# One core, a decoder layer with 32 experts: the overflow branch is named ahead of the first gather

## The chip, the core and the metric

The kernel runs on one core of a Trainium2 chip. A core has five engines that run their own instruction streams in order and meet through semaphores: TensorE (PE, with its weight loads shown as PEld), VectorE (DVE), ScalarE (ACT), GpSimd (POOL) and SyncE (SP), which here only issues transfers. The metric is the device time of one execution in microseconds; the kernel before takes 2275.43 us (median of three runs, 2272.79 to 2275.65).

## The reference

One decoder layer over 2048 tokens of width 1024. Only its mixture of experts is touched here:

```python
h2 = rmsnorm(x, g_ffn[i])
x = x + hier_moe(h2, ...)       # 32 experts: top-1 of 4 groups, then top-2 of its 8 experts
# inside: rows of ht are gathered by expert, in blocks of one expert each
return (jax.nn.silu(xb @ w_eg[e]) * (xb @ w_eu[e])) @ w_ed[e]
# and the rows of each token are summed again, weighted by the router
```

Ahead of it stand a state-space mixer, a windowed attention and their output projection; behind it a gated per-layer embedding and a last RMSNorm.

## The kernel before

All products are made in float32 accuracy out of rounded pieces: each operand is split into a high part, cast by ScalarE (L1488 for weights, L1375 for the gathered rows), and a low part, subtracted by VectorE (L1489 and L1376). A weight unit is 128 x 2048 floats, 1 MB; an expert has six, e0_0 to e0_5 for the expert in place 0, of which 0 to 3 are gate and up and 4 and 5 are down. A unit is loaded by SyncE (`moe_raw`, L1479) into one of four raw buffers and split (`moe_split`) into one of six slots.

The router (`route_tables`) leaves a table of row numbers, `IDX`, and the number of overflow blocks, `NOV`. Places alternate between wide ones, of 128 rows plus up to 96 more (place 0 gathers `s0` and `s32`), and narrow ones of 128 rows (place 31 gathers `s31`). `fetch` calls `moe_in` (L1360 on) for each gather: GpSimd gathers rows by an indirect transfer into one of two buffers `xg` (L1364), TensorE transposes them (L1374), ScalarE and VectorE split them into `xw` (L1375, L1376). The trace calls the gathered tile `xgs`, the transposes `txs`, the expert's raw, high and low weights `e_r`, `e_h` and `e_l`, whatever the place.

`overflow` (L1562 on) holds a branch and a loop over blocks that did not fit; with these inputs there are none, so every engine jumps over the loop. Having jumped, each engine adds to its semaphores what the loop would have added, so that what stands behind the loop and shares a buffer with it (the slots 3 to 5, a raw buffer, an `xg` buffer, two PSUM buffers) waits until the other engine has jumped as well. An engine's stream is not reordered across the branch where a buffer is shared.

What stands in which place of a stream is decided when the program is built, by a scheduler with a timeline of its own. It takes the instructions in the order in which the code names them, moves them where it finds them free earlier, and keeps the order of two users of the same buffer. The engines then run their streams strictly as built.

The first matmuls of the experts are those of `moe_gu_wide` (L1413, L1414): `ws` out of e0_0 and the first half of `xw`, for 224 rows.

Of the kernel before, what the change touches and what calls it, by code (L numbers as in the profile page):

```python
# [43 lines left out]
def more(r):  # L44

    return 32 * ((r < R1) + (r < R3) + (r < R2))


class Kern:
# [1451 lines left out]
    def moe(self):  # L1501
        nc = self.nc
        self.yb_d = self.scratch("yb_d", [2 * T + 1, 1024])

        p = self.mp
        for q in "hl":
            p.tile([128, 8, 128], F32R, tag=f"x{q}", name=f"x{q}at", bufs=1)
        p.tile([128, 512], F32, tag="act", name="aat", bufs=3)
        for q in "hl":
            p.tile([128, 4, 128], F32R, tag=f"a{q}", name=f"a{q}at", bufs=2)  # L1510
        p.tile([128, 4, 2 * RM], F32R, tag="aw", name="awat", bufs=1)
        order = []
        for i in range(16):
            order += [(i, [i, 32 + i]), (31 - i, [31 - i])]

        def number(r):
            return nc.sync.value_load(self.EID[0:1, r:r + 1], min_val=0, max_val=NE - 1)

        def fetch(slots):
            ix = [self.IDX[:, s:s + 1] for s in slots]  # L1520
            if len(slots) == 1:
                return self.moe_in(ix[0], f"s{slots[0]}"), 128
            m = more(slots[0])
            x = self.mp.tile([128, 8, 2, RM], F32R, tag="xw", name=f"xw{slots[0]}", bufs=1)[:, :, :, 0:128 + m]
            for q, (s, w) in enumerate(zip(slots, (128, m))):
                self.moe_in(ix[q], f"s{s}", w, x, 128 * q)
            return x, 128 + m

        self.wslots((), range(3))
        with self.tc.issue_after(self.stored):  # L1530
            v = number(0)
            ahead = [self.moe_raw((v, j), f"e0_{j}") for j in range(3)]
        cur = v, fetch(order[0][1])
        self.wslots(range(3), ())

        with self.tc.issue_after(self.routed[0]), self.tc.issue_after(self.routed[1]):
            ahead = [self.moe_split(w, f"e0_{j}") for j, w in enumerate(ahead)]
        self.wslots(range(3, 6), (3,))
        self.overflow()
        self.rctx.close()  # L1540
        self.wslots((3, 4, 5, 0, 1, 2), range(4))
        prev = None
        for n, (r, slots) in enumerate(order):
            v, xs = cur
            if n + 1 < len(order):
                cur = number(order[n + 1][0]), fetch(order[n + 1][1])
            nm = [f"s{s}" for s in slots]
            wt = ahead + [self.moe_unit((v, j), f"e{r}_{j}") for j in range(len(ahead), 4)]
            ahead = []
            x, rows = xs  # L1550
            wide = rows > 128
            acts = self.moe_gu_wide(x, rows, wt, nm[0]) if wide else self.moe_gu(x, wt, nm[0])
            if prev is not None:
                self.moe_down(*prev())
            hl = acts if wide else self.moe_act(acts, nm[0])

            def prev(v=v, r=r, hl=hl, slots=slots, nm=nm):
                wt = [self.moe_unit((v, j), f"e{r}_{j}") for j in (4, 5)]
                return hl, wt, [self.YDX[:, s:s + 1] for s in slots], nm
        return self.moe_down(*prev())  # L1560
# [231 lines left out]
```

## Time and profile before

| what | value |
| --- | --- |
| median of three runs | 2275.43 us |
| the profiled execution's own time | 2276.06 us |
| its span, first to last instruction | 2274.3 us |
| TensorE busy | 2202.4 us, 97% |
| VectorE busy | 1651.0 us, 73% |
| ScalarE busy | 1208.2 us, 53% |
| GpSimd busy | 364.3 us, 16% |
| mean granted TensorE clock | 0.988 |

The shares of busy time are means over stages of different kinds, so the profile is read by stage: the router's end and the first expert lie between 1276 and 1312 us after the span's start, the experts as a whole between 1297 and 2010 us. A row of a timeline gives start, duration, engine, line, operation, what is written and read, and in brackets the engine's idle time before it with what ended it. A name with a q behind it (PEldq, SPq) is that engine's sequencer: register loads, branches, semaphores and the issue of transfers.

### The profile page before, as it was taken

To read this page: it belongs to the slowest core of one execution; us is meant where nothing else is said; L and a number is where in the kernel's file an instruction comes from. 1 tells how busy PE (TensorE), PEld (TensorE's weight loads), DVE (VectorE), ACT (ScalarE), POOL (GpSimd) and SP (SyncE) were. 2 spreads that over 40 slices of the span, in tenths; PEclk is the share of its full clock that TensorE was granted. 3 is DMA by queue.
4 is the path that set the end of the run, shared out by engine and by line. 5 is a ranking of instruction groups with operands and counts; after the bars stand their busy time and mean duration, and the time that the engine had idled before them with its cause. 6 is when DMAs were issued, how large, how long until landed. Compare 5 with 4: busy or idle time off the path is not lost. (4 is left out here: it accounts for less than half of the span.)

```text
span 2274.3 us, 38003 instructions
## 1 busy us (share of the span) xinstructions
PE 2202.4 (97%) x14524; PEld 1994.3 (88%) x14524; DVE 1651.0 (73%) x2923; ACT 1208.2 (53%) x2011; POOL 364.3 (16%) x281
## 2 busy tenths in 40 slices
PE   8889999999999999999999799999999999999997
PEld 8888997899999999998887688888988888887875
DVE  7978646788786534435666687788888888887997
ACT  6433335567675423322222576666677767774443
POOL 0033200211111000000001211222212222210212
PEclk9989999999999999999999899999999999999998
DMA  8485554643433656645553788889889988986562
GB/s 315 140 278 182 154 153 133 239 156 120 144 126 128 222 165 196 199 135 163 168 167 115 290 306 295 312 324 342 316 314 337 352 325 320 341 298 234 211 203 93
DMA packets 135322, 512.51 MB, mean 225 GB/s; under 512 B 16417, under 2 KB 34769, under 8 KB 107745
## 3 DMA queue, kind: packets, MB, share of 16 engines
q1 hardware_dynamic: 112544, 429.56, 55.3%
q0 software_dynamic: 22448, 80.23, 9.4%
q8 instruction: 115, 1.88, 0.3%
q14 instruction: 71, 0.57, 0.1%
q10 hardware_dynamic: 144, 0.26, 0.0%
HBM read 405.51 MB, written 101.20 MB: 223 GB/s over the span
## 5 line engine op out<-in xcount | busy, mean ns | idle before, releaser
L1489 DVE TENSOR_TENSOR e_l<-e_r,e_h 128x2048 fp32r<-128x2048 f32 x192 | 438.1, 2289 | 136.9 <-ACT e_h L1488 136.1
L1488 ACT CAST e_h<-e_r 128x2048 fp32r<-128x2048 f32 x192 | 366.7, 1911 | 136.0 <-PE ws L1413 40.2
L1413 PE MATMUL ws<-xw,e_h 128*128 128x320 f32 (+2 forms) x1024 | 289.9, 359 | 6.6 <-PEq L1566 6.6
L1414 PE MATMUL ws<-xw,e_l 128*128 128x160 f32 (+2 forms) x1024 | 251.6, 248 | 0.0
L1413 PEld LDWEIGHTS ws<-xw,e_h 128*128 128x128 f32 x1024 | 191.8, 188 | 10.5 <-issue 6.8
L1414 PEld LDWEIGHTS ws<-xw,e_l 128*128 128x128 f32 x1024 | 195.5, 191 | 0.0
L1364 POOL DMA_INDIRECT xgs<-h_d,rt x48 | 87.0, 1812 | 392.6 <-PE txs L1374 366.1
L1464 POOL DMA_INDIRECT yb_d<-yos,rt x48 | 79.1, 1648 | 211.8 <-DVE yos L1460 111.3
L839 POOL TENSOR_TENSOR s<-s,m 128x1024 f32<-128x1024 f32 (+1 forms) x32 | 59.7, 1865 | 313.9 <-DVE m L838 248.1
L77 PE MATMUL pz<-pg_h,pl 128*128 128x512 f32 (+1 forms) x264 | 103.5, 393 | 2.9 <-DVE pl L1627 2.8
L75 PE MATMUL pz<-pg_h,ph 128*128 128x512 f32 (+1 forms) x264 | 102.2, 387 | 0.9 <-ACT ph L1626 0.9
L76 PE MATMUL pz<-pg_l,ph 128*128 128x512 f32 (+1 forms) x264 | 102.0, 386 | 0.0
L75 PE MATMUL gus<-e_h,xhs 128*128 128x512 f32 x256 | 101.3, 396 | 0.0
L77 PE MATMUL gus<-e_h,xls 128*128 128x512 f32 x256 | 101.1, 395 | 0.0
L76 PE MATMUL gus<-e_l,xhs 128*128 128x512 f32 x256 | 99.8, 390 | 0.0
L75 PE MATMUL u<-xh,u_h 128*128 128x256 f32 x256 | 72.3, 288 | 11.3 <-ACT u_h L96 8.3
L836 ACT ACTIVATE s<-s,m 128x256 f32<-128x256 f32 (+1 forms) x128 | 62.8, 492 | 25.4 <-DVE m L832 25.0
L76 PE MATMUL u<-xl,u_h 128*128 128x256 f32 x256 | 72.8, 288 | 3.2 <-DVE xl L422 3.2
L77 PE MATMUL u<-xh,u_l 128*128 128x256 f32 x256 | 72.2, 285 | 0.0
L924 ACT ACTIVATE gt<-gz,bgate 128x256 f32<-128x256 f32 x128 | 53.5, 470 | 28.7 <-PE gz L77 24.0
L1671 POOL TENSOR_TENSOR pth<-pth,gtail 128x1024 f32<-128x1024 f32 x15 | 36.4, 2425 | 176.4 <-ACT pth L1670 151.6
L77 PEld LDWEIGHTS pz<-pg_h,pl 128*128 128x128 f32 x264 | 49.9, 189 | 15.5 <-DVE pl L1627 6.5
(1488 smaller groups left out, 7348.0 us busy)
## 6 DMA issues: line engine op xcount, KB each, us to landing
e_r<-in_We SPq DMA_DIRECT2D x192, 1024.0 KB, 7.3
m_d<-mo SPq DMA_DIRECT2D x64, 256.0 KB, 4.2
yg<-yb_d SPq DMA_DIRECT2D x15, 1024.0 KB, 7.5
xt<-in_xT SPq DMA_DIRECT2D x16, 512.0 KB, 8.7
sq<-in_x SPq DMA_DIRECT2D x16, 512.0 KB, 4.8
m<-m_d SPq DMA_DIRECT2D x16, 512.0 KB, 5.4
xr<-in_x SPq DMA_DIRECT2D x16, 512.0 KB, 4.4
x_d<-xr POOLq DMA_DIRECT2D x16, 512.0 KB, 3.2
```

Of the source, the lines that this page charges most:

```text
L75: mm(out, ah, bh, start=start, stop=False)
L76: mm(out, ah, bl, start=False, stop=False)
L77: return mm(out, al, bh, start=False, stop=stop)
L836: A.activation(s[:, i], s[:, i], AF.Exp, bias=m[:, i:i + 1], accum_out=dn[:, i:i + 1])
L839: nc.gpsimd.tensor_tensor(out=s, in0=s, in1=dn.unsqueeze(2).to_broadcast([128, 4, n]), op=ALU.mult)
L924: A.activation(th[:, m], z[:, m], AF.Tanh, bias=bg[:, q:q + 1], scale=0.5)
L1364: nc.gpsimd.indirect_dma_start(out=xg[0:rows], out_offset=None, in_=self.h2_d[:], in_offset=bass.IndirectOffsetOnAxis(ap=idx[0:rows], axis=0))
L1413: mm(acc[b].rearrange("p (a n) -> p a n", a=2), wh[:, c:c + 128], xk, start=s, stop=False)
L1414: mm(acc[b][:, 0:n], wl[:, c:c + 128], xk[:, 0], start=False, stop=e)
L1464: nc.gpsimd.indirect_dma_start(out=self.yb_d[:], out_offset=bass.IndirectOffsetOnAxis(ap=d[0:rows], axis=0), in_=yo[0:rows], in_offset=None)
L1488: nc.scalar.copy(hi, raw)
L1489: nc.vector.tensor_tensor(out=lo, in0=raw, in1=hi, op=ALU.subtract)
```

## The change

The code names the overflow branch right behind the loads of the first three units, then the gathers of place 0, then the splits of e0_0 to e0_2.

```diff
@@ -1530,13 +1530,13 @@
         with self.tc.issue_after(self.stored):
             v = number(0)
             ahead = [self.moe_raw((v, j), f"e0_{j}") for j in range(3)]
+        self.wslots(range(3, 6), (3,))
+        self.overflow()
         cur = v, fetch(order[0][1])
         self.wslots(range(3), ())
 
         with self.tc.issue_after(self.routed[0]), self.tc.issue_after(self.routed[1]):
             ahead = [self.moe_split(w, f"e0_{j}") for j, w in enumerate(ahead)]
-        self.wslots(range(3, 6), (3,))
-        self.overflow()
         self.rctx.close()
         self.wslots((3, 4, 5, 0, 1, 2), range(4))
         prev = None
```

No instruction is added or removed. SyncE's stream is the same up to the end of the expert stage. On ScalarE, at the end of the router, the four casts of the gathered rows of place 0 (out of `txs00` to `txs321`) stand ahead of the branch in the kernel before; behind the loop (the dots) come two casts of weights, e0_3 and e31_0, and then copies of results:

```order
L1077 COPY po15_14556<-pp151_14565 128x512
L1375 CAST xw0_14614<-txs00_14617 128x4x128
L1375 CAST xw0_14614<-txs01_14624 128x4x128
L1375 CAST xw0_14614<-txs320_14633 128x4x96
L1375 CAST xw0_14614<-txs321_14640 128x4x96
L1565 TENSOR_LOAD rt35_14398
L1566 COMPARE_AND_BRANCH
...
L1566 UNCONDITIONAL_BRANCH
L1488 ACT_TABLE_LOAD
L1488 CAST e0_3_h_14927<-e0_3_r_14925 128x2048
L1488 CAST e31_0_h_15152<-e31_0_r_15150 128x2048
L1420 COPY ts000_15000<-ws000_14932 128x224
```

In the changed kernel ScalarE's stream at the same place, behind the loop, reads:

```order
L1566 UNCONDITIONAL_BRANCH
L1488 ACT_TABLE_LOAD
L1488 CAST e0_3_h_14927<-e0_3_r_14925 128x2048
L1488 CAST e31_0_h_15152<-e31_0_r_15150 128x2048
L1375 CAST xw0_14852<-txs00_14855 128x4x128
L1375 CAST xw0_14852<-txs01_14862 128x4x128
L1488 CAST e31_1_h_15158<-e31_1_r_15156 128x2048
L1375 CAST xw0_14852<-txs320_14871 128x4x96
L1375 CAST xw0_14852<-txs321_14878 128x4x96
L1375 CAST xhs31_14909<-txs310_14911 128x512
```

The casts of the first gathered rows have moved behind the branch, and behind casts of three weight units whose loads are issued after SyncE's own jump. The casts of e0_0 to e0_2 stand ahead of the branch in both. VectorE's stream has the same form; behind the loop it reads, in the changed kernel:

```order
L1566 UNCONDITIONAL_BRANCH
L1489 TENSOR_TENSOR e0_3_l_14928<-e0_3_r_14925,e0_3_h_14927 128x2048
L1489 TENSOR_TENSOR e31_0_l_15153<-e31_0_r_15150,e31_0_h_15152 128x2048
L1376 TENSOR_TENSOR xw0_14852<-txs00_14855,xw0_14852 128x4x128
L1376 TENSOR_TENSOR xw0_14852<-txs01_14862,xw0_14852 128x4x128
L1489 TENSOR_TENSOR e31_1_l_15159<-e31_1_r_15156,e31_1_h_15158 128x2048
L1376 TENSOR_TENSOR xw0_14852<-txs320_14871,xw0_14852 128x4x96
L1376 TENSOR_TENSOR xw0_14852<-txs321_14878,xw0_14852 128x4x96
```

The four subtractions for `xw` stood ahead of the branch before; now two stand behind the second weight subtraction and two behind the third. On TensorE and GpSimd nothing but the four groups of transposes and the two gathers of place 0 has passed the branch; the gather of `s32` now uses the `xg` buffer that the loop uses.

## Rows read from the trace of the kernel before

**Rows 1.** The page's head and first part: span, busy time of the engines

```profile
span 2274.3 us, 38003 instructions
PE 2202.4 (97%) x14524; PEld 1994.3 (88%) x14524; DVE 1651.0 (73%) x2923; ACT 1208.2 (53%) x2011; POOL 364.3 (16%) x281
```

**Rows 2.** Busy time by stretch, the experts from their first matmul

```profile
core 0: us, PE busy (x) PEld busy (x) DVE busy (x) ACT busy (x) POOL busy (x), PEclk, DMA share, GB/s
1297.20:2010.00 712.80, 712.76 (x4132) 626.68 (x4133) 578.65 (x678) 498.40 (x623) 154.56 (x89) 1.00 0.89 325
```

**Rows 3.** TensorE's longest wait from 1297 us on: total, times, longest

```profile
PE ws L1413 <- PEq L1566: 6.6, 1, 6.6
```

**Rows 4.** Timeline of TensorE from the router's last matmuls to the experts

```profile
1277.36 1.48 PE L1341 MATMUL sm<-rt,rt 128*128 128x96 bf16 x31 [0.17 <-ACT rt L1336]
1286.35 1.94 PE L1374 MATMUL txs<-ident,xgs 128*128 128x128 f32 x8 [7.51 <-DMA xgs<-h_d,rt]
1289.15 1.51 PE L1374 MATMUL txs<-ident,xgs 96*128 96x96 f32 x8 [0.86 <-DMA xgs<-h_d,rt]
1297.24 0.71 PE L1413 MATMUL ws<-xw,e_h 128*128 128x448 f32 x1 [6.58 <-PEq L1566]
...
1300.24 0.37 PE L1413 MATMUL ws<-xw,e_h 128*128 128x448 f32 x1
```

**Rows 5.** The branch, line 1566: durations in ns, first and last start

```profile
L1566 PEldq COMPARE_BRANCH  x1: 6786/6786/6786, 1290.3 to 1290.3; - x1
L1566 ACTq COMPARE_BRANCH  x1: 50/50/50, 1291.2 to 1291.2; - x1
...
L1566 PEldq EVENT_SEMAPHORE  x1: 51/51/51, 1297.1 to 1297.1; - x1
```

**Rows 6.** Timeline of ScalarE around the branch

```profile
1290.70 0.48 ACT L1375 CAST xw<-txs 128x384 fp32r<-128x384 f32 x1 [0.16 <-PE txs L1374]
1297.25 1.28 ACT L1488 ACT_TABLE_LOAD   x1 [6.07 <-PEq L1566]
1298.55 3.71 ACT L1488 CAST e_h<-e_r 128x2048 fp32r<-128x2048 f32 x2
...
1307.89 1.92 ACT L1488 CAST e_h<-e_r 128x2048 fp32r<-128x2048 f32 x1
```

**Rows 7.** Timeline of VectorE around and behind the branch

```profile
1290.57 1.20 DVE L1376 TENSOR_TENSOR xw<-txs,xw 128x384 fp32r<-128x384 f32 x2 [0.94 <-ACT xw L1375]
1300.48 4.49 DVE L1489 TENSOR_TENSOR e_l<-e_r,e_h 128x2048 fp32r<-128x2048 f32 x2 [8.71 <-ACT e_h L1488]
...
1309.84 2.29 DVE L1489 TENSOR_TENSOR e_l<-e_r,e_h 128x2048 fp32r<-128x2048 f32 x1 [1.43 <-ACT e_h L1488]
...
1312.35 1.28 DVE L1376 TENSOR_TENSOR xls<-txs,xhs 128x512 fp32r<-128x512 f32 x2
```

**Rows 8.** Weight loads: first issue, those of 1288 to 1293 us, landing times

```profile
1287.42 53.66 SPq L1479 DMA_DIRECT2D e_r<-in_We  x15
...
L1479 SPq DMA_DIRECT2D e_r<-in_We x1: 815/815/815, 1288.0 to 1288.0; - x1
DMA to landing us min/median/max: 10.9/10.9/10.9
...
L1479 SPq DMA_DIRECT2D e_r<-in_We x2: 332/332/333, 1289.1 to 1292.6; - x2
...
DMA to landing us min/median/max: 5.6/7.1/10.9
```

**Rows 9.** Busy time by stretch around the first matmul, columns as in rows 2

```profile
1295.00:1300.00 5.00, 2.76 (x9) 2.61 (x10) 0.00 (x0) 2.73 (x2) 0.93 (x1) 0.50 1.01 418
1300.00:1305.00 5.00, 5.00 (x33) 4.74 (x33) 4.49 (x2) 2.26 (x2) 0.00 (x0) 0.98 0.91 343
```

**Rows 10.** Gathers on GpSimd: that of s32, and the first behind TensorE's jump

```profile
1283.15 1.83 POOL L1364 DMA_INDIRECT xgs<-h_d,rt  x1 [0.30 <-issue]
...
1297.46 0.93 POOL L1364 DMA_INDIRECT xgs<-h_d,rt  x1 [5.58 <-PEq L1566]
```

## The prediction

> **What bounds the kernel now.** I read the page's first part, then busy time by stretch, then the list of waits from the experts on, then the timelines of the engines around the branch. TensorE is busy for 2202.4 of 2274.3 us [rows 1]. From the first expert matmul at 1297.24 us to 2010 us it is busy for 712.76 of 712.80 us [rows 2], and the longest entry in its list of waits from 1297 us to the end is the one just ahead of that first matmul, 6.6 us in one piece [rows 3]. So the experts run on TensorE alone, without a gap: a microsecond by which their first matmul starts later or earlier goes through to the end. The whole question is when that matmul starts.
>
> Before, it starts at 1297.24. TensorE ends the router's matmuls at 1277.36 + 1.48 = 1278.84, waits 7.5 us for the first gather, transposes from 1286.35 to 1290.66, and then jumps over the overflow loop, which holds its sequencer from 1290.3 for 6.786 us [rows 4, 5]. The last subtraction for the gathered rows ends at 1290.57 + 1.20 = 1291.77 [rows 7], 5.5 us ahead of the matmul. So the jump is the last of these waits: two waits, for the gather and for the jump, stand one behind the other.
>
> **The change part by part.** *The jump.* It now follows the router's matmuls directly, while TensorE would wait for rows anyway: 1278.84, less the 0.4 us by which the sequencer began its jump ahead of the end of the last transposes (1290.3 against 1290.66) [rows 4, 5], plus 6.8 is 1285.3, a microsecond ahead of the first gather's landing. By itself this removes up to 6.6 us [rows 3]. If the jump is as short as ScalarE's, 0.05 us [rows 5], it ends earlier still; neither case is on the path found below.
>
> *The gathers.* The first has its row numbers at the same time as before, and the other `xg` buffer. The second, of `s32`, now takes the buffer that the loop uses, so it waits until TensorE has jumped; a gather that waited so was issued at 1297.46, 0.36 us behind the semaphore at 1297.1 [rows 5, 10]. That makes about 1285.6 instead of 1283.15 [rows 10].
>
> *The casts and subtractions of the gathered rows.* This is the term that decides. They used to stand ahead of the branch, where nothing but routing work preceded them. In the new streams of ScalarE and VectorE, two of the four stand behind the splits of e0_3 and e31_0, and two behind the split of e31_1 as well. Those three units are loaded by SyncE, whose stream is unchanged, from 1287.42 on [rows 8]. Queued behind the waiting casts are, in turn, VectorE's subtractions, the second pair of transposes (which need the PSUM buffers of the first pair) and the first expert matmul. The price, step by step:
>
> - e31_0 is issued at 1288.0 and lands 10.9 us later, at 1298.9; it is the second load of that batch [rows 8].
> - Its cast takes 1.9 us (3.71 for two) [rows 6]: 1300.8. VectorE's subtraction, 2.29 [rows 7]: 1303.1.
> - Two subtractions of gathered rows, 1.28 for such a pair [rows 7]: 1304.4. Now the PSUM buffers are free for the transposes of `s32`, some 0.75 us for each half (1.51 for both) [rows 4], with a cast of 0.48 behind each [rows 6]; these run while VectorE does the next step.
> - VectorE subtracts e31_1, 2.29: 1306.7. That unit must have landed and been cast by 1304.4. It is issued at 1289.1, right behind e31_0 [rows 8], and 1 MB at 343 to 418 GB/s [rows 9] is 2.5 to 3.1 us: it lands at 1301.4 to 1302.0, and with 1.92 for the cast [rows 6] it is ready by 1303.9.
> - The first of the two subtractions of 96 rows, 0.6 (1.20 for two) [rows 7]: 1307.3. From its release to the first matmul I take 0.1, as from the semaphore at 1297.1 to 1297.24 [rows 4, 5]: 1307.4.
>
> So the first matmul starts 1307.4 - 1297.24 = 10.2 us later. ScalarE adds a little: it must first have e0_3, with a table load of 1.28 and a cast of 1.9 [rows 6]. If that load lands 2.5 to 3.1 us ahead of e31_0, at 1295.8 to 1296.4, the cast of e31_0 begins at 1299.0 to 1299.6 instead of 1298.9. I add 0.5. The sum is +10.7 us.
>
> *The splits of e0_0 to e0_2.* The code names them later, but on ScalarE and VectorE they stand ahead of the branch as before, and their raw buffers come free at the same times. Price 0; the cover is the wait for the gather, some 7.5 us [rows 4].
>
> *What is late next.* When TensorE does start, e0_0 to e0_3, e31_0 and e31_1 are already split, three units more than before, where e31_1 was cast only at 1307.89, 10.7 us behind the first matmul [rows 6]. I see no new gap: TensorE had none with less in hand [rows 2].
>
> *Bounds of what the trace doesn't show.* The loads could be quicker: with the fastest landing near here, 5.6 us [rows 8], e0_3 is there at 1293.0, and the same chain (1.28, 1.9, 1.9, 2.29, 1.28, 2.29, 0.6, 0.1) ends at 1304.6, +7.4 us. The clock could give something back: before, the granted clock was 0.50 (1.2 GHz) in 1295 to 1300 [rows 9], after little work since 1278.84, and the first matmul took 0.71 us where one at 1300.24 took 0.37 [rows 4]; running 3.0 us at that level costs at most half of it, 1.5. TensorE will again have been nearly idle, so I take 0 of this back, and -1.5 as the end: +5.9 in all. On the other side, the gather of `s32`, 96 x 4 KB = 0.39 MB, now runs among the weight loads, 0 to 1.1 us at 343 GB/s; I take 0, since one gather of 0.5 MB, the one issued at 1297.46 [rows 10], leaves the same stretch. And the trace proves e31_1 landed only by 1307.89 [rows 6]; if it really lands that late, its cast, subtraction and the rest (1.92, 2.29, 0.6, 0.1) end at 1312.8, +15.6 us.
>
> Against the profiled execution's own 2276.06 us (span 2274.3 and 1.8 around it) the sum is 2286.8. That execution lies 0.6 above the median of the runs, 2275.43, so the forecast is 2286.1, rounded to 2286.
>
> **The rivals.** *Faster: the jump is hidden and nothing takes its place.* The place is TensorE's jump. With the gather of `s32` issued at 1285.6 and the 8.6 us that it took before from issue to the last subtraction (1283.15 to 1291.77) [rows 7, 10], the first matmul starts at 1294.3, 2.9 us earlier; with a short jump that no longer holds the gather, at 1291.9, 5.3 us earlier: 2270 to 2273, middle 2271. The point from which it decides: e31_1 must be split before VectorE would subtract the last 96 rows, at 1290.6. For it speaks that the two waits are in series now [rows 4]; against it, that e31_1 is issued only at 1289.1 and the fastest landing here took 5.6 us [rows 8]. Chance 0.04.
>
> The Trainium skill, on its page "Runtime: NRT & Kernel Launch", section "Instruction fetch mechanics", says that a taken branch with a target outside the prefetched window stalls until its page has been fetched. By that rule the jump's length is a fetch that can be laid under any wait, which is this rival. The trace agrees for TensorE (6.786 us against 0.05 on ScalarE [rows 5]) but says nothing of who waits next.
>
> *No change: slack.* The later start could be made up in a stage that waits for something else. Against it: 0.04 us of idle time in 713 [rows 2]. For it: only that three more units are split at the start. 2275.4; chance 0.05.
>
> *Much slower: e31_1 lands late*, or another load pushes itself ahead of it, since the fourth load of the batch, issued at 1292.6 [rows 8], waits for VectorE's jump, which now comes earlier. Up to +15.6, so 2291. Chance 0.10.
>
> *It doesn't do what it says.* For the splits this is so, and priced at 0; the gathers do move.
>
> **How the numbers follow.** Forecast (+5.9 to +14.5 us) 0.81, late 0.10, no change 0.05, faster 0.04. The range 2281 to 2290 is the forecast's: its low end is the bound +5.9, its high end lies short of the late case, and some 0.19 is left out. What a measurement of this kernel can tell from no change is 0.2%, 4.6 us. Slower 0.91, same 0.05, faster 0.04.
>
> **What would show it.** In the new profile: TensorE's jump ahead of the first transposes, ending by 1287; the casts of `xw` on ScalarE behind two casts of weights, at about 1301, where the engine's idle time ends with a landing load; a first L1413 matmul at 1307 to 1308, its wait put down to VectorE's L1376; no gap on TensorE from there to 2010 + 11 us. A first matmul ahead of 1303, a gap later in the experts, or splits of e31_0 done before 1299 would prove the sum wrong.

## The result, and the profile after

The changed kernel takes 2287.43 us (median of five runs, 2283.76 to 2291.13) against 2275.43 us; the ratio is 1.0054, with a 95% interval of 1.0039 to 1.0068, or 12.3 us (8.9 to 15.5). The forecast was 2286, within 2281 to 2290, and slower.

The page's head, as [rows 1]: the span is 11.3 us longer, and TensorE's busy time 3 us.

```profile
span 2285.6 us, 38010 instructions
...
PE 2205.4 (96%) x14524; PEld 1996.7 (87%) x14524; DVE 1649.9 (72%) x2923; ACT 1207.6 (53%) x2011; POOL 366.1 (16%) x281
```

TensorE's list of waits from 1276 us to the end, its longest entries first (total, times, longest). [rows 3] is the same list from 1297 us on:

```profile
PE txs L1374 <- DVE xw L1376: 15.4, 1, 15.4
PE txs L1374 <- DVEq L1566: 7.8, 1, 7.8
...
PE ws L1413 <- DVE xw L1376: 1.7, 1, 1.7
```

The wait for TensorE's own jump is gone from the list. In its place stands one of 15.4 us for VectorE's L1376, the subtractions of gathered rows. The timeline of TensorE, as [rows 4], shows where:

```profile
1275.83 1.48 PE L1341 MATMUL sm<-rt,rt 128*128 128x96 bf16 x31 [0.17 <-ACT rt L1336]
1285.15 1.94 PE L1374 MATMUL txs<-ident,xgs 128*128 128x128 f32 x8 [7.84 <-DVEq L1566]
1302.53 1.54 PE L1374 MATMUL txs<-ident,xgs 96*128 96x96 f32 x8 [15.44 <-DVE xw L1376]
1305.79 0.74 PE L1413 MATMUL ws<-xw,e_h 128*128 128x448 f32 x1 [1.72 <-DVE xw L1376]
...
1309.31 0.38 PE L1413 MATMUL ws<-xw,e_h 128*128 128x448 f32 x1
```

The router's last group starts 1.5 us earlier than in the trace of before. That place moves from 1272 to 1278 us over the traces of this study, whose TensorE streams are alike ahead of it, so I count from it. From the start of that group to the first expert matmul is called the lead-in here: 1305.79 - 1275.83 = 29.96 us, against 1297.24 - 1277.36 = 19.88 before [rows 4]. That is +10.08 us. The second pair of transposes, once 0.9 us behind the first, now waits for PSUM buffers that VectorE frees only at 1302.5.

ScalarE, as [rows 6], and VectorE, as [rows 7], in the order in which their streams have it:

```profile
1294.15 1.28 ACT L1488 ACT_TABLE_LOAD   x1 [11.07 <-DMA e_r<-in_We]
1295.45 3.87 ACT L1488 CAST e_h<-e_r 128x2048 fp32r<-128x2048 f32 x2
1299.22 1.06 ACT L1375 CAST xw<-txs 128x512 fp32r<-128x512 f32 x2
1300.18 1.91 ACT L1488 CAST e_h<-e_r 128x2048 fp32r<-128x2048 f32 x1
1303.47 0.48 ACT L1375 CAST xw<-txs 128x384 fp32r<-128x384 f32 x1 [1.38 <-PE txs L1374]
```

```profile
1297.38 4.49 DVE L1489 TENSOR_TENSOR e_l<-e_r,e_h 128x2048 fp32r<-128x2048 f32 x2 [12.54 <-ACT e_h L1488]
1301.79 1.28 DVE L1376 TENSOR_TENSOR xw<-txs,xw 128x512 fp32r<-128x512 f32 x2
1302.99 2.28 DVE L1489 TENSOR_TENSOR e_l<-e_r,e_h 128x2048 fp32r<-128x2048 f32 x1
1305.18 1.01 DVE L1376 TENSOR_TENSOR xw<-txs,xw 128x384 fp32r<-128x384 f32 x2
```

ScalarE stands idle for 11.07 us until a weight unit lands; that is e0_3, the first that its stream asks for. The first transposes of the rows were done at 1287.1, but their casts stand behind e0_3 and e31_0. From 1294.15 on ScalarE and then VectorE work with hardly a pause, and the first matmul follows the first 96-row subtraction. The load itself, as [rows 8]:

```profile
1286.04 2.51 SPq L1479 DMA_DIRECT2D e_r<-in_We  x4
```

So e0_3 landed 8.1 us behind its issue. The second load, e31_0, was issued at 1286.64 and landed 10.7 us later, at 1297.3, just ahead of its cast at 1297.4. Line 1566, as [rows 5], holds the surprise:

```profile
L1566 PEldq COMPARE_BRANCH  x1: 369/369/369, 1277.3 to 1277.3; - x1
L1566 PEldq EVENT_SEMAPHORE  x1: 51/51/51, 1277.7 to 1277.7; - x1
L1566 ACTq COMPARE_BRANCH  x1: 50/50/50, 1280.6 to 1280.6; - x1
```

TensorE's jump takes 0.369 us where it took 6.786. From the first matmul on the experts are as gapless as in [rows 2]:

```profile
core 0: us, PE busy (x) PEld busy (x) DVE busy (x) ACT busy (x) POOL busy (x), PEclk, DMA share, GB/s
1305.70:2018.50 712.80, 712.71 (x4124) 626.12 (x4125) 571.13 (x677) 491.62 (x619) 155.09 (x89) 1.00 0.87 319
```

Behind the first matmul the changed trace is 2.75 us longer to the end of the span (979.81 against 977.06). Of this 1.05 lies between the first expert matmul and the first transposes of the per-layer stage (L1625), and 1.8 between the first and the last of those. This second stretch lasted 179.9 to 183.5 us over the twelve traces (181.7 before, 183.5 after), and its code is the same in all; I give it no cause.

### The profile page after: what moved, and what is told of

Read it like the earlier page. It is cut to its first block, busy times and chain, and to the rows that moved or that the text cites. A ratio compares the mean times of both kernels' runs of the same rounds, so it can differ in the third digit from the quotient of the medians.

```text
span 2285.6 us, 38010 instructions
## 1 busy us (share of the span) xinstructions
PE 2205.4 (96%) x14524; PEld 1996.7 (87%) x14524; DVE 1649.9 (72%) x2923; ACT 1207.6 (53%) x2011; POOL 366.1 (16%) x281
## 5 line engine op out<-in xcount | busy, mean ns | idle before, releaser
L75 PE MATMUL u<-xh,u_h 128*128 128x256 f32 x256 | 72.0, 287 | 11.3 <-ACT u_h L96 8.3
L1374 PE MATMUL txs<-ident,xgs 128*128 128x128 f32 (+3 forms) x384 | 48.8, 264 | 23.3 <-DVE xw L1376 15.4
L1374 PEld LDWEIGHTS txs<-ident,xgs 128*128 128x128 f32 (+3 forms) x384 | 41.0, 143 | 30.4 <-DVE xw L1376 15.8
```

Source lines behind the costliest of these rows:

```text
L75: mm(out, ah, bh, start=start, stop=False)
L1374: nc.tensor.transpose(tp[:, k], xg[0:rows, kk * 128:kk * 128 + 128], self.ident[0:rows, 0:rows])
```

## The experiments

The theory: the cost is the queue. The casts and subtractions of the gathered rows stand in ScalarE's and VectorE's streams behind splits whose loads SyncE issues only after its own jump. The rivals: the branch ahead of the gather costs by itself, through the jump or the later gathers; and the run time of the splits decides, not their landing. A second question came from the result: why the jump shrank.

All kernels in one table. The jump, the lead-in (as above) and "behind" (from the first expert matmul to the end of the span) come from one traced execution of each kernel; the last two columns are the ratio of its runs to those of the kernel before, with its interval, and the same in us.

| kernel | TensorE's jump, us | lead-in, us | behind, us | ratio | against before, us |
| --- | --- | --- | --- | --- | --- |
| before | 6.79 | 19.88 | 977.06 | 1 | 0 |
| changed | 0.37 | 29.96 | 979.81 | 1.0054 (1.0039 to 1.0068) | +12.3 |
| only the gather moved | 0.37 | 31.05 | 979.28 | 1.0042 (1.0027 to 1.0058) | +9.6 |
| only the splits moved | 6.63 | 19.75 | 976.67 | 0.9999 (0.9989 to 1.0009) | -0.2 |
| one more load | 0.37 | 33.69 | 978.77 | 1.0069 (1.0053 to 1.0085) | +15.7 |
| rows' casts second | 0.37 | 26.84 | 978.73 | 1.0033 (1.0019 to 1.0047) | +7.5 |
| rows' casts first | 0.37 | 23.20 | 978.73 | 1.0011 (1.0002 to 1.0020) | +2.5 |
| and second transposes later | 0.37 | 13.87 | 982.67 | 1.0007 (0.9998 to 1.0016) | +1.6 |
| and evictions ahead of e31_2 | 0.37 | 13.87 | 980.85 | 0.9994 (0.9983 to 1.0004) | -1.4 |
| and evictions ahead of e31_1 | 0.38 | 13.87 | 979.57 | 0.9989 (0.9979 to 1.0000) | -2.5 |
| before, branch shifted | 0.37 | 13.73 | 978.51 | 0.9986 (0.9977 to 0.9995) | -3.2 |
| changed, branch shifted | 3.89 | 29.21 | 979.95 | | 2285.33 in one run |

**Half of the change each.** First the gather alone is named behind the branch:

```diff
-        cur = v, fetch(order[0][1])
         self.wslots(range(3), ())
         ...
         self.overflow()
+        cur = v, fetch(order[0][1])
```

> Half of the change: the first gather of rows is named behind the branch, and the first expert's splits stay named ahead of both, as they were. Theory 1 (the place of the gather alone decides what the scheduler puts ahead of its casts): all of the change's cost, 2287 us (2284 to 2290), first L1413 matmul 30 us behind the start of the router's last matmuls. Theory 2 (the splits' place matters too): between 2276 and 2284 us. On the jump of TensorE: if its length comes from the branch's place among TensorE's instructions, it is again about 0.4 us; if 6.8 and 0.37 us were chance, it is anything from 0.4 to 7.

The lead-in is 31.05 us and the time +9.6 us (6.1 to 13.2): the changed kernel again. Then the splits alone:

```diff
         cur = v, fetch(order[0][1])
-        self.wslots(range(3), ())
-        ...
         self.wslots(range(3, 6), (3,))
         self.overflow()
+        self.wslots(range(3), ())
+        ...
```

> The other half: the first expert's splits are named behind the branch, and the gather stays ahead of it. Theory 1 (the splits' place costs nothing): 2275.4 us (2273 to 2277.5), first L1413 matmul 19.9 us behind the router's last group as before. Theory 2 (splits behind the branch cost a part): 2278 us or more. On the jump of TensorE: 6.8 us again if the branch's place among TensorE's instructions makes it, anything from 0.4 to 7 if chance does.

The lead-in is 19.75 us and the time that of before. So the naming of the splits is worth nothing, as priced, and the gather's place, within the intervals, all of it. The jump's length went with the branch's place both times, 0.369 and 6.626 us.

**The rows' casts first.** `issue_after` fixes an order within an engine's stream, without a semaphore. Here it keeps the splits of e0_3, e31_0 and e31_1 behind the last cast and the last subtraction of the rows; nothing else in the code changes.

```diff
-            nc.scalar.copy(hi[:, 4 * h:4 * h + 4], tp)
-            nc.vector.tensor_tensor(out=lo[:, 4 * h:4 * h + 4], in0=tp, in1=hi[:, 4 * h:4 * h + 4], op=ALU.subtract)
+            self.xin = [nc.scalar.copy(hi[:, 4 * h:4 * h + 4], tp).ins,
+                        nc.vector.tensor_tensor(out=lo[:, 4 * h:4 * h + 4], in0=tp, in1=hi[:, 4 * h:4 * h + 4],
+                                                op=ALU.subtract).ins]
...
+        x0 = self.xin
...
+            with ExitStack() as behind:
+                for i in x0 if n < 2 else ():
+                    behind.enter_context(self.tc.issue_after(i))
-            wt = ahead + [self.moe_unit((v, j), f"e{r}_{j}") for j in range(len(ahead), 4)]
+                wt = ahead + [self.moe_unit((v, j), f"e{r}_{j}") for j in range(len(ahead), 4)]
```

> The changed kernel with one more order on ScalarE and VectorE: the casts and subtractions of the gathered rows (xw) stand ahead of the splits of e0_3, e31_0 and e31_1. Theory 1 (the rows' casts queue behind a split whose load lands late, and nothing else costs): in the changed kernel's trace the first transposes start at 1285.15 and last 1.94, so the casts run from about 1287, the transposes of the 96 rows follow at about 1288.2, and the first L1413 matmul starts at 1290.3 to 1291.2 in place of 1305.79. That is 14.6 to 15.5 us less than the changed kernel: about 2272 to 2273 us, 2 to 4 us under the kernel before, with no wait of TensorE for e0_3 behind it. Theory 2 (the branch standing ahead of the gather costs by itself, by the jump or by the later gathers, whatever stands ahead of the casts): the first matmul stays at 1303 or later, 2284 to 2288 us.

Most of the cost goes, 12.3 to 2.5 us, which no theory of the branch itself allows. But theory 1 had the size wrong: the last 96-row subtraction ended at 1290.4, as expected, and the first matmul started at 1298.97. The timeline of TensorE in this kernel (line 1414 is the former 1413):

```profile
1287.57 1.75 PE L1374 MATMUL txs<-ident,xgs 96*128 96x96 f32 x8 [0.55 <-DVE xw L1376]
1298.23 1.08 PE L1374 MATMUL txs<-ident,xgs 128*128 128x128 f32 x4 [8.91 <-DMA xgs<-h_d,rt]
1298.97 0.72 PE L1414 MATMUL ws<-xw,e_h 128*128 128x448 f32 x1
```

The scheduler had put four transposes of the second round's rows (`s31`) ahead of the first expert matmul, and their gather, issued at 1289.60 among the weight loads, took until 1298.2.

**The rows' casts second.** The same edges for e31_0 and e31_1 only (`n == 1` in place of `n < 2`), so e0_3 stays ahead:

> A smaller dose: only the split of e0_3 stays ahead of the rows' casts, those of e31_0 and e31_1 stand behind them. Theory 1 (the landing of e0_3's load is the gate, and the two later splits add only their own run time): e0_3 is cast at 1295.45 as in the changed kernel, its subtraction ends at 1299.6, two subtractions of rows end at 1300.9, the transposes of the 96 rows at 1302.4, and the first L1413 matmul starts at 1302.8 to 1303.4 in place of 1305.79: 2.4 to 3.0 us less than the changed kernel, about 2284.5 to 2285 us. Theory 2, as the prediction had it (e31_0's and e31_1's loads are the gate): with both behind, the first matmul starts by 1299, 7 us less, about 2280 us.

The lead-in is 26.84 us, 3.1 less than in the changed kernel, where theory 1 said 2.4 to 3.0 and theory 2 about 7. ScalarE in this kernel:

```profile
1296.43 1.28 ACT L1489 ACT_TABLE_LOAD   x1 [11.35 <-DMA e_r<-in_We]
1297.73 1.90 ACT L1489 CAST e_h<-e_r 128x2048 fp32r<-128x2048 f32 x1
1299.53 1.06 ACT L1375 CAST xw<-txs 128x512 fp32r<-128x512 f32 x2
```

So e0_3's landing is a gate by itself; e31_0 and e31_1 add what they take to split.

**One more load ahead of e0_3.**

```diff
         self.rctx.close()
+        self.wslots((), (3,))
+        self.moe_raw((v, 3), "more")
         self.wslots((3, 4, 5, 0, 1, 2), range(4))
```

> The changed kernel with one more 1 MB weight load on SyncE's queue ahead of e0_3's (an input block that nothing uses). ScalarE and VectorE do the same splits and rows' casts ahead of the first expert matmul, in another order among themselves (the first two rows' casts ahead of e31_0's split). Theory 1 (the landing of e0_3 is the gate of the whole chain): it lands later by what 1 MB takes while the queue is full, 2.5 to 3.1 us by the rate of 343 to 418 GB/s seen before, so ScalarE starts it about 11 us behind its issue in place of 8.1, and the first L1413 matmul stands 33 us behind the router's last group in place of 30: 2290 us, 2.5 to 3 more than the changed kernel. Theory 2 (the landing has slack, the splits' run time alone makes the delay): no difference, 2287 us.

SyncE's issues, and what ended ScalarE's wait, in this kernel:

```profile
1285.37 0.35 SPq L1479 DMA_DIRECT2D more_r<-in_We  x1
1285.93 22.44 SPq L1479 DMA_DIRECT2D e_r<-in_We  x7
```

```profile
1296.90 1.28 ACT L1488 ACT_TABLE_LOAD   x1 [14.80 <-DMA e_r<-in_We]
```

e0_3 lands 11.0 us behind its issue in place of 8.1. Counted from the router's last group (1274.84 here) it lands 22.06 us behind in place of 18.32, 3.7 us later, and the lead-in is 3.7 us longer; the time is +15.7 us (12.1 to 19.3) against before. Landing has no slack; the rival is out. The extra load delays e31_0 as well (landed 12.6 us behind its issue), so this kernel doesn't tell the two loads apart.

**The branch shifted in the changed kernel.** 18 tiny matmuls with an unused result, 36 TensorE instructions, behind the router's last group:

```diff
+        for q in range(18):
+            nc.tensor.matmul(bank[:, 256:256 + 2 * NS1], self.la[:, q], mv[:, q].rearrange("p a s -> p (a s)"),
+                             start=True, stop=True)
```

> The changed kernel with 18 tiny matmuls (36 TensorE instructions, result unused) behind the router's last group, which puts the branch back to about the place among TensorE's instructions that it has in the kernel before, while all else of the changed order stays. Theory A (TensorE's jump takes 6.8 us where its place leaves the target outside what the engine holds, and 0.37 us otherwise): 6.6 to 6.8 us again, ending near 1285, with the transposes of the first rows moved by under 1 us and the time as in the changed kernel, 2284 to 2291 us. Theory B (6.8 us came from weight loads on the DMA engines beside the fetch; in the changed kernel these loads start behind the jump): 0.37 to 1 us.

```profile
L1569 PEldq COMPARE_BRANCH  x1: 3886/3886/3886, 1276.3 to 1276.3; - x1
```

3.89 us: long again, as A has it, but not as long as before. ScalarE's second cast of weights here waits for a load, that of e31_0, so the two loads gate almost together:

```profile
1295.41 1.90 ACT L1491 CAST e_h<-e_r 128x2048 fp32r<-128x2048 f32 x1 [0.60 <-DMA e_r<-in_We]
```

The transfers during the jump, in this kernel (1276.3 to 1280.2):

```profile
DMA packets 111, 0.39 MB, mean 101 GB/s; under 512 B 18, under 2 KB 18, under 8 KB 110
...
q8 instruction: 1, 0.02, 2.0%
```

and during the jump of the kernel before (1290 to 1297.2):

```profile
DMA packets 430, 2.74 MB, mean 381 GB/s; under 512 B 42, under 2 KB 42, under 8 KB 151
...
q8 instruction: 1, 0.02, 0.8%
```

Each of the three long jumps has one transfer of queue 8, an instruction queue, beside it, and in all three the jump ends 1.4 us behind the end of that transfer. During the nine short jumps there is none; in the changed kernel the next one starts at 1279.2, behind the jump. The Trainium skill, page "Runtime: NRT & Kernel Launch", section "Instruction fetch mechanics", says that a taken branch outside the prefetched window has to fetch its page first; the three long jumps agree, though no trace shows what lay in the window. The wait lasted 3.89 us in a stretch of 101 GB/s and 6.8 us in one of 381 GB/s. The difference lies ahead of the transfer, which starts 1.2 us behind the start of the jump here and 4.4 us behind it in the kernel before; once started it takes 1.3 and 1.0 us. Whether the traffic holds it back is not shown, since these runs change the place a little as well.

**The rows' casts first, and the transposes of the second round later.** `second` fetches the rows of place 31; its gather and transposes are now named behind the first 20 pairs of expert matmuls:

```diff
...
+                    if second and j == 0 and kh == 1 and b == 0:
+                        with self.tc.issue_after(i.ins):
+                            self.second = second()
...
```

> The kernel with the rows' casts first, and besides that the second round's gather and transposes (s31) are named behind the first 20 pairs of matmuls of the first expert, so TensorE no longer waits for that gather ahead of its first L1413 matmul. Theory 1 (in that kernel all that was left of the cost was the 8.9 us wait for the second round's gather): the rows are ready at 1290.4 where the router's last group starts at 1275.8, so the first expert matmul starts 14.7 us behind that group in place of 19.9 before and 23.2 in the kernel with the casts first: about 5 us less than before, 2270 to 2271.5 us (ratio 0.998). Theory 2 (the loads that are issued late by SyncE, e0_3 above all, take over as the next wait, or the clock returns later): a new wait of TensorE behind the first matmuls gives most of it back, 2274 to 2278 us.

The lead-in falls to 13.87 us, 6.0 below before, and the time doesn't: +1.6 us (-0.5 to 3.6). Theory 2 in part. TensorE has a new wait, and VectorE's timeline says for what (line 1493 is the former 1489, 1425 the former 1421):

```profile
PE ws L1414 <- DVE ts L1425: 3.8, 1, 3.8
```

```profile
1303.29 2.29 DVE L1493 TENSOR_TENSOR e_l<-e_r,e_h 128x2048 fp32r<-128x2048 f32 x1 [1.63 <-ACT e_h L1492]
1306.19 2.29 DVE L1493 TENSOR_TENSOR e_l<-e_r,e_h 128x2048 fp32r<-128x2048 f32 x1 [0.60 <-ACT e_h L1492]
1308.40 0.38 DVE L1425 TENSOR_TENSOR ts<-ws,ts 128x224 f32<-128x224 f32 x1
```

The first eviction of results stands behind splits that wait for loads: the same pattern, one step later. The clock pays too (busy time by stretch, columns as in [rows 2]):

```profile
1304.90:1308.80 3.90, 0.10 (x2) 0.00 (x0) 3.30 (x4) 3.88 (x7) 0.00 (x0) 1.00 0.99 326
1308.80:1310.30 1.50, 1.47 (x8) 1.20 (x8) 1.50 (x4) 1.49 (x3) 0.00 (x0) 0.94 1.03 431
1310.30:1313.40 3.10, 3.10 (x12) 2.86 (x11) 2.57 (x3) 2.39 (x5) 0.00 (x0) 0.50 0.97 404
```

Behind the 3.8 us wait TensorE runs 1.3 us at 2.4 GHz and then 3.4 us at 1.2 GHz (granted clock 1.00 from 1308.83 to 1310.13, and 0.50 from there to 1313.55).

**Evictions ahead of the later splits.** Besides all this, the splits of e31_2 and later stand behind the evictions of the first half (first kernel), or those of e31_1 and later (second, `j == 1`); `evicted` holds the last copy and addition of that half:

```diff
...
+                    if n == 1 and j == 2:
+                        for i in self.evicted:
+                            behind.enter_context(self.tc.issue_after(i))
...
```

> As the kernel with the evictions first, but only the splits of e31_2 and later stand behind the evictions; TensorE's order is then exactly that of the kernel without this edge. Theory 1: VectorE's subtraction for e31_1 ends at 1305.6, the first eviction follows at once, so TensorE's wait ends near 1306.1 in place of 1308.8 and lasts about 1.2 us in place of 3.8, with no or a shorter dip of the clock: 2.6 to 4 us less than without the edge, 2270 to 2271.5 us. Theory 2: no gain, as above, 2273 to 2276 us.

> The kernel with the rows' casts first and the second round's transposes later, and besides that the splits of e31_1 and later on ScalarE and VectorE stand behind the evictions (L1424, L1425) of the first expert's first half. Theory 1 (TensorE's 3.8 us wait, for VectorE's first eviction at 1308.40, and the slower clock behind it are the whole of what was given back): both go, about 5 us less than that kernel, 2268 to 2270 us (ratio 0.997 to 0.998 against before). Theory 2 (the weight loads bound this stretch: the DMA engines are at 1.01 busy in every window from 1289 to 1312): TensorE waits for the second expert's weights next, near 1318 in the frame of that kernel, and the time stays within 2 us of before, 2273 to 2276 us.

The dose shows in the trace: the wait of 3.8 us becomes 1.1 in the first kernel and is gone in the second. The times don't separate the two: medians of 2271.86 and 2272.46 us against 2274.31 for before beside them, -1.4 us (-3.9 to 0.9) and -2.5 us (-4.8 to 0.0) by the ratios. Theory 1 is right about the wait and too hopeful about the time: it had 2270 to 2271.5 us for the first kernel and 2268 to 2270 for the second. No wait for the second expert's weights appears, so the mechanism of theory 2 is out. What is missing in the second kernel lies behind the lead-in, 979.57 us against 977.06. The start of the experts in the second kernel, by stretch:

```profile
1286.83:1290.00 3.17, 3.17 (x11) 2.95 (x12) 0.56 (x1) 0.21 (x1) 0.91 (x1) 0.50 1.00 386
1290.00:1293.00 3.00, 3.00 (x13) 2.79 (x13) 0.93 (x1) 1.90 (x1) 0.00 (x0) 0.57 1.00 418
1293.00:1296.00 3.00, 3.00 (x22) 2.86 (x21) 1.49 (x2) 1.91 (x1) 0.00 (x0) 1.00 1.04 427
```

The first matmul at full speed starts at 1292.73, 5.9 us behind the first one, where before it was 3.0 [rows 4]. At half the clock about half of the difference is lost time, an estimate of 1.4 us. The other 1.1 us I can't place.

**The branch shifted in the kernel before.** 112 such tiny matmuls, 224 TensorE instructions, in the time in which TensorE waits for the first gather; nothing else changes:

```diff
         done = self.row_index(ip, t([128, NS1]), self.IDX, self.YDX)
+        for q in range(112):
+            nc.tensor.matmul(bank[:, 256:256 + 2 * NS1], self.la[:, q % 32], mv[:, q % 32].rearrange("p a s -> p (a s)"),
+                             start=True, stop=True)
```

> The kernel before, with 112 tiny matmuls (224 TensorE instructions, result unused, about 0.05 us each) behind the router's last group, in the 7.5 us in which TensorE waits for the first gather; nothing else in the order changes, the branch only stands 224 instructions further on in TensorE's stream. 224 is one fetched block of 16 KB (256 instructions of 64 bytes, if the one transfer in the instruction queue beside the long jump is such a block) less the 32 instructions by which the change brought the branch forward. Theory A (place alone makes the long jump): 0.37 us in place of 6.79, so the first L1413 matmul starts when the rows are ready, near 1292 in the frame of the kernel before, 5.3 us sooner; if nothing else comes late that is 2270 us, if the evictions behind late splits give it back as in the kernel with the transposes later, 2273 to 2276 us. Theory B (traffic alone makes it long): 6.6 to 6.8 us again and 2275 us.

```profile
L1569 PEldq COMPARE_BRANCH  x1: 369/369/369, 1285.8 to 1285.8; - x1
```

```profile
1273.16 1.48 PE L1341 MATMUL sm<-rt,rt 128*128 128x96 bf16 x31 [0.18 <-ACT rt L1336]
1275.18 4.92 PE L1346 MATMUL sm<-rt,rt 128*128 128x96 bf16 x112 [0.54 <-DVE rt L1356]
1282.03 1.06 PE L1377 MATMUL txs<-ident,xgs 128*128 128x128 f32 x8 [1.94 <-DMA xgs<-h_d,rt]
1284.95 1.42 PE L1377 MATMUL txs<-ident,xgs 96*128 96x96 f32 x8 [1.86 <-DMA xgs<-h_d,rt]
1286.89 0.74 PE L1416 MATMUL ws<-xw,e_h 128*128 128x448 f32 x1 [0.52 <-DVE xw L1379]
```

The jump is 0.369 us, although it comes as late as before and beside the same loads (400 GB/s from 1283 to 1290.2): the place decides whether it is long, and such traffic doesn't. The first matmul comes 13.73 us behind the router's group, 6.15 less than before, and the kernel is faster than before by 3.2 us (1.1 to 5.2). The useless matmuls gain nothing by the clock: the first transposes do take 1.06 us in place of 1.94, but those of the 96 rows wait for their gather and start 11.79 us behind the group in both kernels [rows 4]. Here too a part goes behind the lead-in: again about 5 us at 1.2 GHz, and a gap of 0.98 us without a releaser, from 1291.3 to 1292.3. That gap ends 1.4 us behind the end of a transfer of queue 8, as the long jumps do, which suggests a fetch here as well and doesn't show it.

## Why the prediction was right

The forecast held, and by its own mechanism.

*Which wait ends last.* Right. The chain of the sum is the chain of the trace, and its steps fit. Shifted by the 1.38 us by which SyncE's first load is earlier (1287.42 and 1286.04), the sum with its 0.5 us for ScalarE reads, against the trace: e31_0 subtracted at 1302.2 (1301.9), the first rows' subtractions done at 1303.5 (1303.1), e31_1 subtracted at 1305.8 (1305.3), first matmul at 1306.5 (1305.79). The lead-in grew by 10.1 us where +10.7 was said.

*Which load is the gate.* The sum began with e31_0's landing, 10.9 us behind its issue, and gave e0_3 only 0.5 us. In the trace e0_3 is what ScalarE waits for, and e31_0, 10.7 us behind its issue, has landed 0.1 us before its turn comes; in the changed kernel with the branch shifted ScalarE waits for it by 0.60 us. So the two paths are as close as the sum had them, and the size survived the wrong name. The kernel "rows' casts second" shows that e0_3 alone still holds the lead-in at 26.84 us. The late landing of e31_1, the rival, did not happen: its cast at 1300.18 waits for no load.

*The jump.* Mis-sized: 6.8 us taken, 0.37 measured, because moving the branch 32 instructions forward also took away its fetch. It was said that neither length lies on the path, and so it was. The gather of `s32`, which was to wait for the jump until 1285.6, went at 1281.64 instead, off the path as well. A wait that I had not listed, the first transposes' 7.84 us for VectorE's jump behind three weight subtractions, cost nothing: they start 9.32 us behind the router's group where the gather let them start at 8.99 before, and the casts of their rows stand until 1299.2 behind e0_3 and e31_0.

*The splits of e0_0 to e0_2.* 0, shown by the kernel that moves them alone.

*The clock.* No gain from it, as taken: 3.5 us from the first matmul to the first at full speed, against 3.0.

*The faster rival.* Its mechanism is real: the jump and the gather were two waits in series, and either hiding the first (evictions ahead of e31_1) or shortening it (the branch shifted in the kernel before) cuts the lead-in by 6 us. It was priced at 2.9 to 5.3 us in the end time; 2.5 (0.0 to 4.8) and 3.2 (1.1 to 5.2) were measured, with more time behind the lead-in, of which the clock explains a part. What kept it from happening here was the point named for it: units split too late ahead of the rows' subtractions.

*What the sum left out.* The time grew by 12.3 us (8.9 to 15.5) and the lead-in by 10.1; one traced execution has 2.75 more behind the lead-in, of which no experiment isolates a cause.

## What to carry to other kernels

Moving a wait under another wait is worth nothing if the move also changes what stands ahead in the other engines' in-order streams: write down, for each engine, what the next result now queues behind, and when the load of that lands. Here one order for two engines decided 10 us, and each repair uncovered the next such queue (casts behind splits, transposes behind a gather, evictions behind splits). A length read from one execution, such as that of a jump, belongs to the place where it was read.

## What the runs showed of the hardware

A taken branch on TensorE took 0.37 to 0.38 us in nine of these kernels and 6.79, 6.63 and 3.89 us in three. Beside each of the three lies one transfer in the instruction queue, and the jump ends 1.4 us behind it; 32 to 36 instructions of shift are enough to bring it about. That 112 useless matmuls could make a kernel faster was the plainest sign of it.

The time at 1.2 GHz differs from start to start. From the first expert matmul to the first at full speed it was 3.0 us before, 3.5 in the changed kernel, and 3.7, 4.8 and 5.9 us in the three kernels whose lead-in was 13.87, so the lead-in doesn't set it; with the branch shifted in the kernel before it was 5.4, a gap of 1 us included. In the kernel with the transposes later the clock fell once more, 1.3 us after the end of a wait of 3.8 us, for 3.4 us.
